# Attention on one core: VectorE's order by hand, P.V in three blocks of six key tiles, maxima moved by F32R matmuls

## The chip, the cores and the metric

The kernel runs on one core of a Trainium2 chip (8 cores, one used here). The metric is the device time of one execution in microseconds (us), as the median of repeated runs; lower is better. The engines of a core are TensorE (PE in the profile, its weight loads apart as PEld), VectorE (DVE), ScalarE (ACT), GpSimd (POOL) and SyncE (SP, which only issues transfers here). Each has its own queue and runs it in order; they meet at semaphores.

## The reference, cut to what matters

The whole computation is a two-layer backbone on 2048 latent and 256 context tokens: an RWKV-7 layer, then a latent-attention layer. The change touches the softmax attention of the second layer alone, 16 heads, 2048 queries against 2304 keys:

```python
def attend(q, k, v):        # q: 2048 x 16 x 96, k: 2304 x 16 x 96, v: 2304 x 16 x 64
    s = jnp.einsum('bqhd,bkhd->bhqk', q, k, preferred_element_type=jnp.float32) * (1.0 / math.sqrt(QK_NOPE + QK_ROPE))
    p = jax.nn.softmax(s, axis=-1).astype(v.dtype)
    return jnp.einsum('bhqk,bkhd->bqhd', p, v, preferred_element_type=jnp.float32).astype(q.dtype)
...
d_x = (o * jax.nn.silu(g_x)) @ w_out
```

Everything is float32. The kernel keeps that precision by splitting operands into a high and a low F32R part (F32R is a float32 format that TensorE takes in one pass) and adding products.

## The kernel before

`attention` works on 32 **groups**: 8 pairs of heads (`p`) times 4 blocks of 512 queries (`g`). The list `work` holds them in order. In a group a loop runs over 18 key tiles of 128 keys (`kt`). For each key tile `scores` (L1699) issues five pairs of matmuls into `ps_s` (two buffers), one matmul of a pair for each head, and ScalarE takes the exponential into a tile `pt` (L1708; nine buffers). Called **S** below.

The maxima that softmax subtracts are found one group ahead. `prepass` (L1668) is a generator that `next(bg, None)` advances: each of its 18 **units** (called **U**) multiplies queries by 512 keys into two `ps_p` tiles, one for each head (three buffers of `ps_p` in all), and VectorE reduces each to a maximum (L1684, L1686). After the 18 units VectorE reduces to `zm` (L1688), eight small float32 matmuls turn those columns into rows (L1694, called **M**), and ScalarE and then VectorE copy one row each into `qr2` (L1697). The last of the five score matmul pairs of the next group reads `qr2`, which is how the maximum is subtracted.

P.V is `av(st, n)` (L1724): the next `n` key tiles of the group, two float32 matmuls each, accumulated in the one buffer of `ps_o`. The group's calls are five tiles at `kt` 6, five at `kt` 11, six after the loop, and the last two in `finish_group` (L1790), which runs inside the next group at `kt` 1.

The row sums of the exponentials are added up elementwise by two engines in `accumulate` (L1711): VectorE adds key tiles 1, 3, 7, 11 and 15 into `acc1` (four instructions), GpSimd the other thirteen into `acc0` (twelve), and then GpSimd adds `acc1` to `acc0` (L1832). `finish_group` calls `av`, `scaled` (multiplies P.V by the gate, L1733) and `sums` (L1735): two matmuls with ones sum `acc0` over the keys, ScalarE copies the result (L1742), VectorE takes the reciprocal in four pieces of 128 columns (L1745) and multiplies (L1747), and SP sends the result off.

What sets the order: `manual_schedule(engines={PE})` keeps TensorE's instructions in the order in which the code is written. VectorE, ScalarE, GpSimd and SP are ordered by the scheduler of the language at build time, by its own priorities. [...] A buffer that is still being read holds up the instruction that wants to write it: a unit needs two of the three `ps_p` buffers, and those come free by VectorE's reductions.

## Time and profile before

| | us |
|---|---|
| median of 3 runs | 5520.99 (5520.9 to 5532.2) |
| profiled execution | 5527.81 |
| its span, first to last instruction | 5526.0 |
| one steady group of attention, from its first S to the next group's | 52.84 |
| last group, from its first S to its sums | 46.05 |

| engine over the span | busy us | share |
|---|---|---|
| PE | 4724.3 | 85% |
| DVE | 3784.7 | 68% |
| POOL | 2752.4 | 50% |
| ACT | 2186.3 | 40% |

Attention lies between about 3620 and 5325 us of the span; what lies ahead of it (RWKV, projections) and behind it (the output product and the final norm) is not touched. The busy shares are means over all stages. What an edit in attention is worth has to be read from a group: it repeats 32 times with nearly the same timing, so one of them, from 4525.33 to 4578.17, is read closely. In the timeline a row gives the start, the time until the last instruction of the row ended, and how many instructions it merges; since matmuls overlap, the distance of two starts is what a step costs.

### The profile page before, as it was taken

What the parts mean: (1) busy time and instruction counts of PE and PEld (TensorE: products, weight loads), DVE (VectorE), ACT (ScalarE), POOL (GpSimd) and SP (SyncE); (2) the same over time, 40 slices, a digit from 0 to 9 for tenths busy, and PEclk for the clock granted to TensorE, in tenths of its full rate; (3) what the DMA queues carried; (4) which work ended last, traced back from release to release, by engine and by line L of the source; (5) the groups of instructions that cost most, each with busy time, mean ns of one, the idle gap of its engine ahead of it and who ended that gap; (6) DMA issues with size and microseconds to landing.
All of it is one profiled execution on the core that took longest, in us unless ns stands there. A gap on an engine that the chain in (4) does not pass through costs nothing.

```text
span 5526.0 us, 123424 instructions
## 1 busy us (share of the span) xinstructions
PE 4724.3 (85%) x50559; PEld 3434.1 (62%) x50559; DVE 3784.7 (68%) x6213; ACT 2186.3 (40%) x3862; POOL 2752.4 (50%) x2473
## 2 busy tenths in 40 slices
PE   6778787887878887677789998699999999999999
PEld 4655555555767776466667876555555555555567
DVE  5989897875888888786565443266666666666644
ACT  4444444443544444333333343233333333333332
POOL 2575656463544444343254452255656655656551
PEclk8889898887989999788889999889999999999999
DMA  7655555556776666868788767621111111011023
GB/s 220 188 168 171 162 165 172 165 169 188 212 214 175 186 178 168 243 196 235 229 247 256 246 163 237 235 76 54 30 50 58 28 51 57 23 58 32 25 91 104
DMA packets 1006881, 818.59 MB, mean 148 GB/s; under 512 B 280885, under 2 KB 876420, under 8 KB 994794
## 3 DMA queue, kind: packets, MB, share of 16 engines
q1 hardware_dynamic: 872046, 734.48, 44.5%
q10 hardware_dynamic: 134188, 75.95, 5.0%
q8 instruction: 397, 6.50, 0.5%
q14 instruction: 170, 1.39, 0.1%
q0 software_dynamic: 80, 0.26, 0.0%
HBM read 551.84 MB, written 258.66 MB: 147 GB/s over the span
## 4 chain that ended last, share of the span: by engine, by line
PE 31%; DVE 9%; DMA 3%; ACT 2%; issue 2%; POOL 2%; SPq 1%; ACTq 0%; DVEq 0%; POOLq 0%
PE ps_o L1729 9%; PE ps_s L1706 7%; PE ps_p L1680 4%; DVE mx L1684 3%; DVE ri L1745 2%; DVE acc L1722 1%; PE ps_a L1387 1%; PE ps_a L1388 1%; PE ps_a L1389 1%; ACT pt L1708 1%; PE ps_o L1882 1%; PE ps_o L1884 1%; PE ps_o L1883 1%; DVE acc L1719 1%; PE ps_p L1694 1%
## 5 line engine op out<-in xcount | busy, mean ns | idle before, releaser
L1722 POOL TENSOR_TENSOR acc<-acc,pt 128x1024 f32<-128x1024 f32 x352 | 867.2, 2464 | 406.5 <-ACT pt L1708 386.5
L1684 DVE TENSOR_REDUCE mx<-ps_p 128x1 f32<-128x512 f32 x1024 | 661.5, 682 | 356.8 <-PE ps_p L1680 356.7
L1708 ACT ACTIVATE pt<-ps_s 128x1024 f32<-128x1024 f32 x576 | 591.0, 1026 | 779.8 <-PE ps_s L1706 737.6
L1706 PE MATMUL ps_s<-qr,a_kr 64*128 64x512 f32 (+1 forms) x2304 | 524.6, 393 | 5.8 <-ACT qr L1697 4.0
L1729 PE MATMUL ps_o<-pt,av 128*64 128x512 f32 x2304 | 523.3, 599 | 0.0
L1680 PE MATMUL ps_p<-knh,qnh 64*128 64x512 f32 (+1 forms) x1280 | 369.9, 404 | 99.3 <-DVE mx L1684 48.9
L500 PE MATMUL ps_r<-lh,whi 128*128 128x512 f32 (+1 forms) x960 | 386.4, 404 | 37.0 <-ACT lh L492 33.4
L418 POOL TENSOR_TENSOR wlo<-wraw,whi 128x1024 fp32r<-128x1024 f32 (+3 forms) x120 | 265.7, 2215 | 300.2 <-ACT whi L414 293.8
L501 PE MATMUL ps_r<-ll,whi 128*128 128x512 f32 (+1 forms) x960 | 382.7, 400 | 15.4 <-DVE ll L493 11.9
L502 PE MATMUL ps_r<-lh,wlo 128*128 128x512 f32 (+1 forms) x960 | 379.6, 397 | 12.9 <-POOL wlo L418 7.1
L696 POOL TENSOR_TENSOR f_wlo<-f_wraw,f_whi 128x384 fp32r<-128x384 f32 x118 | 158.8, 1347 | 384.4 <-ACT f_whi L694 320.0
L1729 PEld LDWEIGHTS ps_o<-pt,av 128*64 128x64 f32 x2304 | 154.3, 137 | 296.3 <-issue 292.2
L1680 PE MATMUL ps_p<-a_kr,qr 64*128 64x512 f32 (+1 forms) x1280 | 329.5, 391 | 1.5 <-DMA qr<-qr 1.5
L1706 PEld LDWEIGHTS ps_s<-qr,a_kr 64*128 64x128 f32 (+1 forms) x2304 | 289.9, 185 | 64.3 <-DVE qr L1697 15.2
L1680 PEld LDWEIGHTS ps_p<-knh,qnh 64*128 64x128 f32 x1280 | 184.3, 189 | 196.8 <-DVE mx L1684 132.2
L480 DVE SCALAR_TENSOR_TENSOR lerp<-xx,cols,hb 128x512 f32<-128x512 f32 (+1 forms) x240 | 239.3, 1022 | 88.2 <-POOL ll L493 67.9
L1706 PE MATMUL ps_s<-qnh,knl 64*128 64x512 f32 x1152 | 283.0, 417 | 4.3 <-ACT pt L1708 4.2
L1150 PE MATMUL ps_s<-svu,big 128*64 128x64 f32 x4544 | 236.7, 247 | 52.0 <-DVE svu L1138 30.3
L1706 PE MATMUL ps_s<-qnh,knh 64*128 64x512 f32 x1152 | 267.5, 389 | 0.0
L1706 PE MATMUL ps_s<-qnl,knh 64*128 64x512 f32 x1152 | 267.4, 389 | 0.0
L1097 DVE TENSOR_TENSOR big<-ps_aa,amask 64x256 f32<-64x256 f32 x576 | 243.2, 422 | 29.7 <-PE ps_aa L1092 16.3
L1110 ACT COPY big<-ps_aa 64x256 f32<-64x256 f32 x576 | 211.0, 366 | 132.2 <-PE ps_aa L1106 126.2
(342 smaller groups left out, 12550.1 us busy)
## 6 DMA issues: line engine op xcount, KB each, us to landing
f_w<-wod SPq DMA_DIRECT2D x72, 1024.0 KB
wraw<-rwkv_w_in SPq DMA_DIRECT2D x120, 512.0 KB
kbt<-KB SPq DMA_DIRECT2D x72, 512.0 KB
big<-AR SPq DMA_DIRECT2D x144, 256.0 KB
AR<-ar SPq DMA_DIRECT2D x64, 512.0 KB
KB<-kb SPq DMA_DIRECT2D x64, 512.0 KB
f_wraw<-rwkv_w_in SPq DMA_DIRECT2D x64, 512.0 KB
f_wraw<-mla_w_in SPq DMA_DIRECT2D x54, 512.0 KB
```

What stands on the lines that cost most here:

```text
L418: eng.tensor_tensor(lo[:, k0:k1, :], raw[:, k0:k1, :], hi[:, k0:k1, :].bitcast(F32), ALU.subtract)
L480: nc.vector.scalar_tensor_tensor(L[:, :W], xx[:, k, :W], col["mu"][:, j * 8 + k:j * 8 + k + 1], hb[:, k, 1:W + 1], ALU.mult, ALU.add)
L500: nc.tensor.matmul(ps, hi[:, k, :], lh[k][:, :W], start=k == 0, stop=False)
L501: nc.tensor.matmul(ps, hi[:, k, :], ll[k][:, :W], start=False, stop=False)
L502: nc.tensor.matmul(ps, lo[:, k, :], lh[k][:, :W], start=False, stop=k == KT - 1)
L1097: nc.vector.tensor_tensor(B[r, 2 * p0 + e::4, 0, ck], ps[e][o], amask[o, d:d + 1, :].to_broadcast([64, 4, 64]), ALU.mult)
L1680: nc.tensor.matmul(ps[h2][:, o * kw:(o + 1) * kw], x[r, t * P:(t + 1) * P], y[r, k0:k0 + kw], start=st, stop=not st)
L1684: nc.vector.tensor_reduce(mx[:, h2, t, n % 4:n % 4 + 1], ps[h2], mybir.AxisListType.X, ALU.max)
L1706: nc.tensor.matmul(ps[:, h2, :], x[r, ks], y[r, :], start=i == 0, stop=i == 4)
L1708: nc.scalar.activation(pt, ps, AF.Exp, scale=SCALE)
L1722: eng.tensor_tensor(a, a, pt, ALU.add)
L1729: nc.tensor.matmul(st["po"][hs, :], st["v"][:, kt, hs], pt[:, h2, :], start=kt == 0, stop=kt == NK - 1)
```

## The change

- VectorE joins TensorE in `manual_schedule`: its instructions now keep the order of the code.
- P.V comes in three blocks of six key tiles: at `kt` 7, at `kt` 13 and, for the last six, at `kt` 1 of the next group. Behind each block one more unit of the prepass is issued, so that its 18 units end at `kt` 14 and M comes at `kt` 16 of the same group.
- `sums` of the group before moves from `kt` 1 to `kt` 7, just ahead of the block there. ScalarE's copy goes; VectorE takes one reciprocal of 512 columns straight from PSUM.
- VectorE adds only key tiles 10, 11 and 12 (two instructions), at `kt` 13 in front of the block there. GpSimd adds the other fifteen (fourteen instructions) and then `acc1`. `acc1` has one buffer in place of two.
- M: `zm` becomes a tile of 4 x 128 columns, zero but for two columns of each 128 (two such tiles, cleared once by GpSimd), and four F32R matmuls with an F32R identity (`a_idr`) replace the eight float32 ones.

```diff
@@ -1639,10 +1639,16 @@
             qp = es2.enter_context(tc.tile_pool(name="at_q", bufs=2))
             tp = es2.enter_context(tc.tile_pool(name="at_t", bufs=2))
             pp = es2.enter_context(tc.tile_pool(name="at_ps", bufs=1, space=PSUM))
-            es2.enter_context(tc.manual_schedule(engines={mybir.EngineType.PE}))
+            es2.enter_context(tc.manual_schedule(engines={mybir.EngineType.PE, mybir.EngineType.DVE}))
             wl = cp.tile([P, KT - WC, 2, D], F32R, name="a_wl")
             ones = rp.tile([P, 64], F32, name="a_ones")
             nc.vector.memset(ones, 1.0)
+            idr = rp.tile([P, P], F32R, name="a_idr")
+            nc.vector.tensor_copy(idr, self.ident)
+            zms = [rp.tile([P, 4, P], F32R, name=f"zm{i}") for i in range(2)]
+            for z in zms:
+                nc.gpsimd.memset(z.bitcast(F32), 0.0)
+            zms = itertools.cycle(zms)
             kr1 = rp.tile([P, T], F32R, name="a_kr1")
             kr2 = rp.tile([P, T], F32R, name="a_kr2")
 
@@ -1667,7 +1673,7 @@
 
             def prepass(q, k):
                 qnh, _, qr1, qr2 = q
-                z = tp.tile([P, 8], F32, name="zm")
+                z = next(zms)
                 mx = tp.tile([P, 2, 4, 5], F32, name="mx")
                 units = [[(t, j * 512, 512)] for t in range(4) for j in range(4)]
                 units += [[(t, 2048, 256), (t + 1, 2048, 256)] for t in (0, 2)]
@@ -1685,13 +1691,11 @@
                         else:
                             nc.vector.tensor_reduce(mx[:, h2, t:t + 2, 4], ps[h2].rearrange("p (t k) -> p t k", t=2), mybir.AxisListType.X, ALU.max)
                     yield
-                nc.vector.tensor_reduce(z, mx.rearrange("p h t j -> p (h t) j"), mybir.AxisListType.X, ALU.max, negate=True)
+                nc.vector.tensor_reduce(z[:, :, 32::64].rearrange("p t h -> p h t"), mx, mybir.AxisListType.X, ALU.max, negate=True)
                 yield
                 pz = pp.tile([P, 512], F32, name="ps_p", bufs=3)
                 for t in range(4):
-                    for h2 in range(2):
-                        o = 32 + 64 * h2
-                        nc.tensor.matmul(pz[o:o + 1, t * P:(t + 1) * P], z[:, 4 * h2 + t:4 * h2 + t + 1], self.ident, start=True, stop=True)
+                    nc.tensor.matmul(pz[:, t * P:(t + 1) * P], z[:, t, :], idr, start=True, stop=True)
                 for h2 in range(2):
                     o = 32 + 64 * h2
                     (nc.vector.tensor_copy if h2 else nc.scalar.copy)(qr2[o:o + 1, :], pz[o:o + 1, :])
@@ -1708,18 +1712,16 @@
                 nc.scalar.activation(pt, ps, AF.Exp, scale=SCALE)
                 return pt
 
-            def accumulate(st, kt, pt):
-                if kt < 2:
-                    st["first"].append(pt)
-                    return
-                j = 1 if kt % 4 == 3 else 0
-                eng = nc.vector if j else nc.gpsimd
-                if j not in st["acc"]:
-                    a = st["acc"][j] = tp.tile([P, 2, QG], F32, name=f"acc{j}")
-                    eng.tensor_tensor(a, st["first"][j], pt, ALU.add)
-                else:
-                    a = st["acc"][j]
-                    eng.tensor_tensor(a, a, pt, ALU.add)
+            def add(st, eng, j, *pts):
+                for pt in pts:
+                    a = st["acc"].get(j)
+                    if a is None:
+                        a = st["acc"][j] = tp.tile([P, 2, QG], F32, name=f"acc{j}", bufs=2 - j)
+                        st["first"][j] = pt
+                    elif j in st["first"]:
+                        eng.tensor_tensor(a, st["first"].pop(j), pt, ALU.add)
+                    else:
+                        eng.tensor_tensor(a, a, pt, ALU.add)
 
             def av(st, n):
                 for _ in range(n):
@@ -1739,10 +1741,7 @@
                 for h2 in range(2):
                     nc.tensor.matmul(psm[h2 * 64:(h2 + 1) * 64, :], ones, a[:, h2, :], start=True, stop=True)
                 ri = tp.tile([P, QG], F32, name="ri", bufs=1)
-                nc.scalar.copy(ri, psm)
-                for i in range(4):
-                    c = slice(i * P, (i + 1) * P)
-                    nc.vector.reciprocal(ri[:, c], ri[:, c])
+                nc.vector.reciprocal(ri, psm)
                 ot = st["ot"]
                 nc.vector.tensor_tensor(ot, ot, ri, ALU.mult)
                 (nc.sync if (p, g) != (NP - 1, NG - 1) else nc.gpsimd).dma_start(self.oT[p, :, g * QG:(g + 1) * QG], ot)
...
 
-            def finish_group(st):
-                av(st, len(st["pend"]))
-                scaled(st)
-                sums(st)
-
             for i, (p, g) in enumerate(work):
                 q, k, v = nq, kv, kv[2]
                 gt = tp.tile([P, QG], F32, name="gt")
                 nc.sync.dma_start(gt, self.mG[p, :, g * QG:(g + 1) * QG])
-                st = {"pg": (p, g), "v": v, "gt": gt, "pend": [], "first": [], "acc": {}}
+                st = {"pg": (p, g), "v": v, "gt": gt, "pend": [], "first": {}, "acc": {}}
                 bg = iter(())
                 if i + 1 < len(work):
                     if g + 1 == NG:
@@ -1806,11 +1800,14 @@
                 for kt in range(NK):
                     pt = scores(kt, q, k)
                     st["pend"].append((kt, pt))
-                    accumulate(st, kt, pt)
+                    if kt not in (10, 11, 12):
+                        add(st, nc.gpsimd, 0, pt)
                     next(bg, None)
                     if kt == 1:
                         if prev:
-                            finish_group(prev)
+                            av(prev, 6)
+                            scaled(prev)
+                            next(bg, None)
                         if i + 2 < len(work):
                             fq = load_q(*work[i + 2])
                     if kt == 2 and g == 0:
@@ -1824,17 +1821,23 @@
                             wg = wout_split(range(WC))
                     if kt >= 3:
                         next(wg, None)
-                    if kt == 6:
+                    if kt == 7:
+                        if prev:
+                            sums(prev)
                         st["po"] = pp.tile([P, QG], F32, name="ps_o")
-                        av(st, 5)
-                    if kt == 11:
-                        av(st, 5)
+                        av(st, 6)
+                        next(bg, None)
+                    if kt == 13:
+                        add(st, nc.vector, 1, *(x[1] for x in st["pend"] if x[0] in (10, 11, 12)))
+                        av(st, 6)
+                        next(bg, None)
                 nc.gpsimd.tensor_tensor(st["acc"][0], st["acc"][0], st["acc"][1], ALU.add)
-                av(st, 6)
                 for _ in bg:
                     pass
                 prev = st
-            finish_group(prev)
+            av(prev, 6)
+            scaled(prev)
+            sums(prev)
             for _ in wg:
                 pass
             es2.close()
```

VectorE in the middle of attention, before: one group in the order in which it runs. `mx` is the prepass's maxima, `acc` the sums of exponentials, `ri` the reciprocal, `ot` the group's output.

```order
L1688 TENSOR_REDUCE zm<-mx 128x8
L1697 CAST qr_44048<-ps_p 1x512
L1684 TENSOR_REDUCE mx<-ps_p 128x1 x4
L1733 TENSOR_TENSOR ot<-ps_o,gt 128x512
L1745 RECIPROCAL ri<-ri 128x128 x4
L1684 TENSOR_REDUCE mx<-ps_p 128x1
L1747 TENSOR_TENSOR ot<-ot,ri 128x512
L1684 TENSOR_REDUCE mx<-ps_p 128x1 x2
L1719 TENSOR_TENSOR acc_45056<-pt 128x1024
L1684 TENSOR_REDUCE mx<-ps_p 128x1 x8
L1722 TENSOR_TENSOR acc_45056<-acc_45056,pt 128x1024
```

The same engine and place in the changed kernel:

```order
L1694 TENSOR_REDUCE zm_43773<-mx 128x2x4
L1701 CAST qr_44528<-ps_p 1x512
L1690 TENSOR_REDUCE mx<-ps_p 128x1 x4
L1735 TENSOR_TENSOR ot<-ps_o,gt 128x512
L1690 TENSOR_REDUCE mx<-ps_p 128x1 x14
L1744 RECIPROCAL ri<-ps_p 128x512
L1746 TENSOR_TENSOR ot<-ot,ri 128x512
L1690 TENSOR_REDUCE mx<-ps_p 128x1 x14
L1722 TENSOR_TENSOR acc_45765<-pt 128x1024
L1724 TENSOR_TENSOR acc_45765<-acc_45765,pt 128x1024
L1692 TENSOR_REDUCE mx<-ps_p 128x2 x4
```

The reciprocal moved from behind 4 reductions of a group to behind 18, and the adds, once spread among the reductions, now stand together behind the 32nd.

TensorE around the sums (`a_ones`), before. `ps_p<-knh,qnh` and the row behind it are one unit, the five `ps_s` rows one S.

```order
L1680 MATMUL ps_p<-knh,qnh 128x512 x2
L1680 MATMUL ps_p<-a_kr_43770,qr_47899 128x512 x2
L1729 MATMUL ps_o<-pt,av 64x512 x4
L1740 MATMUL ps_p<-acc_47919,a_ones 64x512 x2
L1706 MATMUL ps_s<-qnh,knl 128x512 x2
L1706 MATMUL ps_s<-qnl,knh 128x512 x2
L1706 MATMUL ps_s<-qr_47419,a_kr_43770 128x512 x2
L1706 MATMUL ps_s<-qnh,knh 128x512 x2
L1706 MATMUL ps_s<-qr_47420,a_kr_43771 128x512 x2
L1680 MATMUL ps_p<-knh,qnh 128x512 x2
```

TensorE around the sums in the changed kernel:

```order
L1686 MATMUL ps_p<-knh,qnh 128x512 x2
L1686 MATMUL ps_p<-a_kr_43776,qr_47830 128x512 x2
L1742 MATMUL ps_p<-acc_47774,a_ones 64x512 x2
L1731 MATMUL ps_o<-pt,av 64x512 x12
L1686 MATMUL ps_p<-knh,qnh 128x512 x2
L1686 MATMUL ps_p<-a_kr_43776,qr_47830 128x512 x2
L1710 MATMUL ps_s<-qnh,knl 128x512 x2
```

Behind the sums there now stands a block of twelve P.V matmuls, where an S and a unit stood.

TensorE around M in the changed kernel (before, M stood between the last P.V block of a group and the next group's first S):

```order
L1710 MATMUL ps_s<-qr_46418,a_kr_43777 128x512 x2
L1698 MATMUL ps_p<-a_idr,zm_43772 128x128 x4
L1710 MATMUL ps_s<-qnh,knl 128x512 x2
L1710 MATMUL ps_s<-qnl,knh 128x512 x2
L1710 MATMUL ps_s<-qr_46417,a_kr_43776 128x512 x2
L1710 MATMUL ps_s<-qnh,knh 128x512 x2
L1710 MATMUL ps_s<-qr_46418,a_kr_43777 128x512 x2
L1710 MATMUL ps_s<-qnh,knl 128x512 x2
```

M now has the whole last S of its group (`qr_46418`) between itself and the next group's first S.

## Rows read from the trace of the kernel before

**Rows 1.** The page: busy time, share and instructions of each engine.
```profile
PE 4724.3 (85%) x50559; PEld 3434.1 (62%) x50559; DVE 3784.7 (68%) x6213; ACT 2186.3 (40%) x3862; POOL 2752.4 (50%) x2473
```
**Rows 2.** All instructions of M: ns min/median/max, first and last start.
```profile
L1694 PE MATMUL ps_p<-ident,zm x512: 270/272/417, 3621.5 to 5270.0; 128*1 128x128 f32 x171
```
**Rows 3.** Two stretches: us, busy PE, PEld, DVE, ACT, POOL, clock, DMA, GB/s.
```profile
4525.33:4578.17 52.84, 50.80 (x355) 30.74 (x353) 34.94 (x48) 19.63 (x20) 31.78 (x14) 1.00 0.11 28
5270.17:5316.22 46.05, 42.52 (x267) 21.75 (x265) 15.62 (x12) 19.63 (x20) 34.92 (x14) 1.00 0.02 7
```
**Rows 4.** TensorE's timeline through the steady group: start, us, instructions, idle before.
```profile
4525.33 0.51 PE L1706 MATMUL ps_s<-qnh,knl 64*128 64x512 f32 x2
...
4529.32 1.94 PE L1729 MATMUL ps_o<-pt,av 128*64 128x512 f32 x8
...
4532.05 0.49 PE L1706 MATMUL ps_s<-qnh,knl 64*128 64x512 f32 x2
...
4536.77 0.49 PE L1680 MATMUL ps_p<-knh,qnh 64*128 64x512 f32 x1 [1.47 <-DVE mx L1684]
...
4543.40 4.51 PE L1729 MATMUL ps_o<-pt,av 128*64 128x512 f32 x20
4547.85 0.49 PE L1706 MATMUL ps_s<-qnh,knl 64*128 64x512 f32 x2
...
4556.86 4.51 PE L1729 MATMUL ps_o<-pt,av 128*64 128x512 f32 x20
4561.31 0.49 PE L1706 MATMUL ps_s<-qnh,knl 64*128 64x512 f32 x2
...
4563.03 0.39 PE L1706 MATMUL ps_s<-qnh,knl 64*128 64x512 f32 x2
...
4564.64 0.39 PE L1706 MATMUL ps_s<-qnh,knl 64*128 64x512 f32 x2
...
4571.90 5.37 PE L1729 MATMUL ps_o<-pt,av 128*64 128x512 f32 x24
4577.20 1.04 PE L1694 MATMUL ps_p<-ident,zm 128*1 128x128 f32 x16
4578.17 0.50 PE L1706 MATMUL ps_s<-qnh,knl 64*128 64x512 f32 x2
```
**Rows 5.** The chain of waits through the same group: start, us, what.
```profile
4525.44 0.59 ACT qr L1697
...
4526.06 0.71 DVE qr L1697
...
4532.16 0.60 ACT ri L1742
...
4532.78 3.39 DVE ri L1745 x4
```
**Rows 6.** VectorE's timeline, the same group.
```profile
4550.43 1.23 DVE L1722 TENSOR_TENSOR acc<-acc,pt 128x1024 f32<-128x1024 f32 x1
...
4557.62 2.92 DVE L1722 TENSOR_TENSOR acc<-acc,pt 128x1024 f32<-128x1024 f32 x1 [0.18 <-ACT pt L1708]
...
4564.84 1.29 DVE L1684 TENSOR_REDUCE mx<-ps_p 128x1 f32<-128x512 f32 x2 [0.32 <-PE ps_p L1680]
```
**Rows 7.** GpSimd's timeline, the same group.
```profile
4552.14 7.32 POOL L1722 TENSOR_TENSOR acc<-acc,pt 128x1024 f32<-128x1024 f32 x3 [4.95 <-ACT pt L1708]
```
**Rows 8.** All instructions on `acc`: ns min/median/max, first and last start.
```profile
L1722 POOL TENSOR_TENSOR acc<-acc,pt x352: 2347/2382/3256, 3641.2 to 5311.4; 128x1024 f32<-128x1024 f32 x176
...
L1722 DVE TENSOR_TENSOR acc<-acc,pt x96: 1224/1244/2975, 3653.4 to 5304.4; 128x1024 f32<-128x1024 f32 x96
```
**Rows 9.** All instructions on `ot`, the multiplication by the reciprocal.
```profile
L1747 DVE TENSOR_TENSOR ot<-ot,ri x32: 691/884/1348, 3692.4 to 5322.1; 128x512 f32<-128x512 f32 x32
```
**Rows 10.** Groups by form, VectorE: a reciprocal of 512 columns elsewhere in the kernel.
```profile
L1359 DVE RECIPROCAL mt<-mt 128x512 f32<-128x512 f32 x8 | 26.8, 3352 | 2.5 <-ACT mt L1358 2.5
```
**Rows 11.** TensorE's timeline at the end of attention: the last group's sums.
```profile
5316.22 1.83 PE L1740 MATMUL ps_p<-acc,a_ones 128*64 128x512 f32 x4 [3.37 <-POOL acc L1832]
```

## The prediction

> **What bounds the kernel now.** The page gives TensorE 85% of the span, VectorE 68%, GpSimd 50%, ScalarE 40% [rows 1]: TensorE leads, but a mean over stages prices nothing. So the next view is the instructions of M, one block of 16 in each of 32 groups: from the first start, 3621.5, to the last, 5270.0, lie 31 groups, 53.2 us each in the mean [rows 2]. The reader is to see that attention repeats, so that a saving counts 31 times. Third, the stretches: a steady group takes 52.84 us, with TensorE busy 50.80, VectorE 34.94, GpSimd 31.78, ScalarE 19.63, the granted clock at 1.00 (2.4 GHz) [rows 3]. Busy 50.80 looks like no room. The timeline shows that it is not so, because waiting matmuls are drawn long.
>
> I take the pace of undisturbed work from that timeline and lay it against the group. One S with its unit U takes 4564.64 - 4563.03 = **1.61**. A P.V block of five tiles takes 4547.85 - 4543.40 = 4.45, one of six 4577.20 - 4571.90 = **5.30**. M takes 4578.17 - 4577.20 = 0.97 [rows 4]. Between the blocks lie these stretches:
>
> - 4525.33 to 4529.32, two S+U: 3.99 for 3.22 of work, 0.77 lost.
> - 4532.05 to 4543.40, five S+U: 11.35 for 8.05, **3.30** lost.
> - 4547.85 to 4556.86, five: 9.01 for 8.05, 0.96 lost.
> - 4561.31 to 4571.90, six: 10.59 for 9.66, 0.93 lost.
>
> Together 5.96 us of 52.84 are not work. The chain of waits and the VectorE timeline name them. The 3.30: behind the sums ScalarE copies for 0.60 and VectorE takes four reciprocals for 3.39 [rows 5]; a unit's maxima stand behind them in VectorE's queue, so its `ps_p` buffers stay taken and TensorE waits for `mx` at 4536.77 [rows 4]; an add to `acc` follows. The 0.96 and 0.93: one VectorE add of about 1.23 in the middle of a stretch [rows 6]; VectorE needs 1.29 of every 1.61 for two reductions, so a delay is worked off slowly. The 0.77: the first S of a group waits for the two copies of the maxima, 0.59 on ScalarE and then 0.71 on VectorE [rows 5]. So the bound is TensorE's work plus holes made by VectorE's order; VectorE's 34.94 in total would fit.
>
> **The change part by part.**
>
> *The sums at `kt` 7 ahead of a block.* In VectorE's queue: two reductions of the unit before (done about 1.5 us after that unit ends, by the 0.32 of idle and 1.29 of [rows 6]), the reciprocal of 512 columns, 3.35 by the row of such an instruction [rows 10], and the multiplication, 0.69 to 1.35 [rows 9]. They end 5.5 to 6.2 after the unit. TensorE has in the same time the sums (0.96, from 4577.20 back: the two-tile block and the sums fill 4529.32 to 4532.05, and two tiles are 1.77) and the block (5.30): 6.26. The next unit's first result comes 0.5 later. So the reciprocal hides behind P.V, which asks nothing of VectorE. That the source is PSUM and not SBUF no row shows; 3.35 is the value taken, and up to 4.3 would still fit. Without the cover it would cost the 3.3 of today. ScalarE's copy of 0.60 goes from the path. Gain: **3.30**.
>
> *The three adds of VectorE in front of the block at `kt` 13.* Two instructions of 1.24 alone, up to 2.98 beside GpSimd [rows 8]: with the reductions ahead of them 1.5 + 2.5 = 4.0 to 7.5 after the unit, against 5.30 of block plus 0.5 of unit. GpSimd has one add, of tile 13, ready there, so one is held and one runs alone: 1.5 + 2.9 + 1.24 = 5.6. Hidden. The spread adds are gone: gain **0.96 + 0.93**.
>
> What the trace shows of a held add is the 2.92 us at 4557.62, while GpSimd's run of three adds lasts until 4559.46; from there it needs 1.08, and alone it takes 1.23 [rows 6, 7]. The Trainium skill, page "SBUF — State Buffer", section "Who interferes with whom", says that a VectorE instruction with two SBUF inputs contends with a GpSimd instruction that reads SBUF, the loser waiting for the whole instruction. The trace agrees; the rule speaks against this change, which fills GpSimd's queue, and what it would make of the time is the first rival.
>
> *M at `kt` 16.* 18 calls in the loop and three behind the blocks make 21; the 18 units end at `kt` 14, `zm` follows at 15, M at 16. Between M and the next group's first S lies the last S of the group. The two copies, 0.59 and 0.71 in a row, have that S (a unit is two of the seven matmul pairs in the 1.61, 0.46; an S is the other 1.15) and four fifths of the next to hide in. Gain: **0.77**. M itself: 16 passes at 0.97 today are 0.06 each. Four F32R matmuls could be four such passes, 0.24; a stationary operand of 128 columns in place of one could cost more, and I let it go to today's 0.97, or to nothing below. I take 0.5, halfway, as no row has this shape: gain **0.47**.
>
> *Blocks of six.* The work is the same 18 tiles. The first S behind a block today takes 4563.03 - 4561.31 = 1.72, that is 0.11 more than the pace [rows 4]; there are four such places in either kernel, so 0.44 of the 5.96 stays. Entering a block may cost as much: I leave 0.2.
>
> *GpSimd.* 15 instructions in place of 13, 2.38 each [rows 8]: 35.7 in a group of about 47, or 76%. Its last one must end before the sums at `kt` 7. Laid out by hand: the adds of tiles 14 to 17 and the final one start when tile 14's exponential is done, some 3 us before the group ends (three S, M), and take 11.9, so they end about 9 us into the next group; the sums stand at 18.7 (eight S+U are 12.9, the block 5.3, one unit 0.5). Ten us to spare. The same lag decides on the nine `pt` buffers: a tile's buffer is wanted nine tiles on, and GpSimd is at most six behind.
>
> *What remains.* VectorE's multiplication by the reciprocal has two SBUF inputs and now meets a GpSimd that rarely rests; held for up to one add, 2.4, it would end 0.9 to 1.0 late, of which a third is absorbed. I leave 0.35 a group.
>
> New group: 52.84 - 5.96 = 46.88, plus 0.44, minus 0.47, plus 0.2 and 0.35: **47.4**. Saving 5.44.
>
> *The ends.* 29 of the 31 groups are steady: 29 x 5.44 = 158. Two groups are longer (31 x 53.2 - 31 x 52.84 is about 11 together), by the weight splits on ScalarE and GpSimd that fall there; I leave those 11 untouched. The later of the two saves as the rest, 5.4; the first has no group before it, so no reciprocal, and I give it 2. The last group has no units and is bound by GpSimd: its sums waited 3.37 for the final add [rows 11], 46.05 after its first S [rows 3]. Now tile 14 comes behind fifteen S, three blocks and the sums, at about 36, and five instructions of 2.38 follow it, with about 1.2 of holds by VectorE: 49, 3 later than 46.05. Without ScalarE's copy 0.6 comes back: minus 2.4.
>
> Sum: 158 + 5.4 + 2 - 2.4 = **163**. On the profiled execution, 5527.8, that is 5365. That execution lies 6.8 above the median of the runs, 5521.0, of which nothing shows the place; against the median it is **5358**.
>
> **The rivals.**
>
> *VectorE is held by GpSimd (slower than the forecast, still faster than before).* Place: the two adds at `kt` 13 and the multiplication behind the reciprocal. If each waits for a whole GpSimd add of 2.38, the adds end 1.5 + 2 x 3.62 = 8.7 after the unit against 6.0 wanted, 2.7 late, and the multiplication 1.0 late. About 0.6 of it is absorbed, so 3.1 a group in place of the 0.35: saving 2.7, in all some 80, 5441. Halfway, with one add held, 5400. For it: the 2.92, and GpSimd's 76%. Against: GpSimd has only tile 13 to add there. The rule of the Trainium skill named above, taken in full, is this rival.
>
> *GpSimd becomes the bound (slower than before).* Place: the sums' matmuls at `kt` 7, in front of all that TensorE has behind them. 15 instructions must fit in a group. At 47.4 us that decides from 3.16 us an instruction, and the kernel gets slower than before from 52.84 / 15 = 3.52. At 3.6 a group takes 54.0, 1.2 more, 36 in all: 5557. For it: single adds took up to 3.256 [rows 8]. Against: the median is 2.382, and only three VectorE instructions a group can hold GpSimd.
>
> *The cover shifts the holes but does not close them (no change).* VectorE by hand is fixed to one order; if the reductions of the seven units between two blocks came late each time, 7 x 1.29 = 9.0 in 10.1 of TensorE's work, the stretches would keep some 5 us of waits. Against: four S+U in a row run at 1.61 with VectorE idle 0.32 before each pair [rows 6].
>
> **How the numbers follow.** The forecast, 5335 to 5385 with 5358 most likely: 0.68. The first rival, 5385 to 5445: 0.20. GpSimd as the bound and slower: 0.04. No change: 0.03. Better than 5335 (M for nothing, no hold at all: a group of 46.3, saving 6.5, 195 in all, 5326): 0.05. The range of 8 in 10 takes the forecast and the nearer half of the first rival, with a little below: 5332 to 5420. Faster by over 0.2%, about what a measurement of this kernel can tell from no change: 0.68 + 0.20 + 0.05 = 0.93; same 0.03; slower 0.04.
>
> **What would show it.** In the changed kernel's profile: steady groups of 47 to 48; TensorE's idle time for `mx` gone; the reciprocal one instruction of about 3.35, ended before the block at `kt` 7 does; VectorE's adds at 1.24 to 3; M at 0.2 to 1.0 with no wait for `qr` behind it; GpSimd near 36 to 38 a group and TensorE not waiting for `acc` except at the very end. Wrong would make it: a reciprocal from PSUM beyond 4.3, waits of S for ScalarE where no units stand between (`kt` 15 to 17), or `pt` buffers that come free late.

## The result and the profile after

The changed kernel takes **5362.2 us** (5361.6 to 5367.7, 4 runs) against 5520.9 (5517.4 to 5532.2, 4 runs): a ratio of 0.9711, 95% interval 0.9695 to 0.9728, 159 us faster. The forecast was 5358 in 5332 to 5420. Its profiled execution took 5361.6, with a span of 5359.8.

The page's engine line, which answers to [rows 1]:

```profile
PE 4623.4 (86%) x50175; PEld 3437.2 (64%) x50175; DVE 3726.7 (70%) x6054; ACT 2167.4 (40%) x3830; POOL 2885.2 (54%) x2539
```

Two stretches, the steady group from its first S to the next one's and the last group from its first S to its sums, as [rows 3]:

```profile
4473.97:4521.32 47.35, 47.35 (x342) 30.59 (x340) 33.05 (x44) 19.06 (x19) 36.03 (x16) 1.00 0.12 32
5100.30:5150.17 49.87, 45.36 (x283) 22.74 (x279) 11.54 (x7) 19.50 (x19) 46.28 (x19) 1.00 0.02 6
```

The steady group fell from 52.84 to 47.35; the forecast was 47.4. TensorE's timeline through it, as [rows 4]: M, the first pair of matmuls that reads the new maxima row, the next P.V block, the unit behind it, the sums with their block, the unit behind that, the third block and the last unit:

```profile
4472.13 0.66 PE L1698 MATMUL ps_p<-a_idr,zm 128*128 128x128 f32 x4
4474.89 0.44 PE L1710 MATMUL ps_s<-qr,a_kr 33*128 33x512 f32 x2
4477.37 5.37 PE L1731 MATMUL ps_o<-pt,av 128*64 128x512 f32 x24
4482.68 0.50 PE L1686 MATMUL ps_p<-knh,qnh 64*128 64x512 f32 x2
4493.05 1.08 PE L1742 MATMUL ps_p<-acc,a_ones 128*64 128x512 f32 x4
4499.21 0.50 PE L1686 MATMUL ps_p<-knh,qnh 64*128 64x512 f32 x2
4509.56 5.37 PE L1731 MATMUL ps_o<-pt,av 128*64 128x512 f32 x24
4514.86 0.39 PE L1686 MATMUL ps_p<-knh,qnh 64*128 64x256 f32 x2
```

From 4482.68 to 4493.05 lie one unit and six S+U: 10.37 us for 0.46 + 6 x 1.61 = 10.12 of work. From 4499.21 to 4509.56 lie the same: 10.35. The long stretch of [rows 4] that lost 3.30 has no successor; each stretch now loses 0.2 to 0.3. VectorE's timeline, as [rows 6], with its copy of the maxima row and then the second and third block:

```profile
4473.96 0.70 DVE L1701 CAST qr<-ps_p 1x512 fp32r<-1x512 f32 x1 [2.51 <-ACT qr L1701]
4493.12 1.29 DVE L1690 TENSOR_REDUCE mx<-ps_p 128x1 f32<-128x512 f32 x2 [0.32 <-PE ps_p L1686]
4494.33 3.35 DVE L1744 RECIPROCAL ri<-ps_p 128x512 f32<-128x512 f32 x1
4497.71 0.90 DVE L1746 TENSOR_TENSOR ot<-ot,ri 128x512 f32<-128x512 f32 x1
4499.98 1.29 DVE L1690 TENSOR_REDUCE mx<-ps_p 128x1 f32<-128x512 f32 x2 [1.36 <-PE ps_p L1686]
4510.86 3.01 DVE L1722 TENSOR_TENSOR acc<-pt 128x1024 f32<-128x1024 f32 x1
4513.98 1.23 DVE L1724 TENSOR_TENSOR acc<-acc,pt 128x1024 f32<-128x1024 f32 x1
4515.64 1.29 DVE L1692 TENSOR_REDUCE mx<-ps_p 128x2 f32<-128x512 f32 x2 [0.43 <-PE ps_p L1686]
```

and, of GpSimd's timeline, the final add of the group before:

```profile
4480.53 2.35 POOL L1834 TENSOR_TENSOR acc<-acc,acc 128x1024 f32<-128x1024 f32 x1
```

Reciprocal and multiplication end at 4498.61, ahead of the block (4499.21), and VectorE then waits 1.36 for TensorE. Of the two adds one is held to 3.01 and one runs alone; behind them VectorE still waits 0.43. The copy of the maxima row ends at 4474.66, and the matmuls that read it start at 4474.89, in step with the pairs ahead of them. Around the blocks VectorE idles only for TensorE, and TensorE never waits for VectorE.

### The profile page after: what moved, and what is told of

It reads as the page before. It is cut to its first block, busy times and chain, and to the rows that moved or that the text cites. A ratio compares the mean times of both kernels' runs of the same rounds, so it can differ in the third digit from the quotient of the medians.

```text
span 5359.8 us, 122473 instructions
## 1 busy us (share of the span) xinstructions
PE 4623.4 (86%) x50175; PEld 3437.2 (64%) x50175; DVE 3726.7 (70%) x6054; ACT 2167.4 (40%) x3830; POOL 2885.2 (54%) x2539
## 5 line engine op out<-in xcount | busy, mean ns | idle before, releaser
L1724 POOL TENSOR_TENSOR acc<-acc,pt 128x1024 f32<-128x1024 f32 x416 | 1003.1, 2411 | 356.3 <-ACT pt L1712 333.6
L1710 PE MATMUL ps_s<-qr,a_kr 64*128 64x512 f32 (+1 forms) x2304 | 474.2, 392 | 0.3 <-DVE qr L1701 0.2
L1686 PE MATMUL ps_p<-knh,qnh 64*128 64x512 f32 (+1 forms) x1280 | 274.7, 399 | 37.4 <-DMA qnl<-qn 33.3
L1686 PE MATMUL ps_p<-a_kr,qr 64*128 64x512 f32 (+1 forms) x1280 | 260.4, 379 | 1.7 <-DMA qr<-qr 1.7
L1710 PEld LDWEIGHTS ps_s<-qr,a_kr 64*128 64x128 f32 (+1 forms) x2304 | 235.2, 185 | 38.4 <-DVE qr L1701 0.5
L500 PEld LDWEIGHTS ps_r<-lh,whi 128*128 128x128 f32 x960 | 197.7, 206 | 92.3 <-ACT lh L492 39.4
L1710 PE MATMUL ps_s<-qnh,knl 64*128 64x512 f32 x1152 | 241.0, 402 | 12.2 <-ACT pt L1712 12.0
L1150 PEld LDWEIGHTS ps_s<-svu,big 128*64 128x64 f32 x4544 | 193.9, 156 | 86.0 <-DVE svu L1138 40.9
L501 PEld LDWEIGHTS ps_r<-ll,whi 128*128 128x128 f32 x960 | 198.0, 206 | 59.6 <-DVE ll L493 19.7
```

Of the source, the lines that this page charges most:

```text
L500: nc.tensor.matmul(ps, hi[:, k, :], lh[k][:, :W], start=k == 0, stop=False)
L501: nc.tensor.matmul(ps, hi[:, k, :], ll[k][:, :W], start=False, stop=False)
L1150: nc.tensor.matmul(ps[e * 64:(e + 1) * 64, h // 2, :], B[:, h, 1, k:k + 64], S[:, e, h // 2, :], start=True, stop=True)
L1686: nc.tensor.matmul(ps[h2][:, o * kw:(o + 1) * kw], x[r, t * P:(t + 1) * P], y[r, k0:k0 + kw], start=st, stop=not st)
L1710: nc.tensor.matmul(ps[:, h2, :], x[r, ks], y[r, :], start=i == 0, stop=i == 4)
L1724: eng.tensor_tensor(a, a, pt, ALU.add)
```

## The experiments

The start of attention differs from run to run (the first M at 3615.3 in the changed kernel's trace, 3607.8 to 3626.1 in the eleven kernels below), and that comes from the program ahead of it. So the kernels are laid beside each other by their groups too, each from its first M to the next group's first M, worked out from the starts of M in each trace. 29 of the 31 intervals are regular; the first interval and the one of the first group of the last head pair (the "long" one) are not. "Group" is the mean of the regular intervals, "31 groups" the sum of all, and "tail" runs from the last M to the last sums.

```
kernel                       median us  ratio to before (95%)    group   31 groups  tail
before                        5520.9    -                         52.77   1647.7     47.0
changed                       5362.2    0.9711 (0.9695-0.9728)    47.38   1483.1     51.7
sums at key tile 4            5483.0    0.9927 (0.9913-0.9942)    51.23   1601.8     52.1
before, sums at tile 6        5467.9    0.9903 (0.9888-0.9918)    51.04   1593.1     47.0
VectorE's adds spread         5434.6    0.9844 (0.9828-0.9861)    49.78   1555.0     51.7
VectorE by the scheduler      5380.5    0.9744 (0.9730-0.9759)    48.00   1502.4     51.7
M behind the last tile        5405.6    0.9786 (0.9772-0.9799)    48.70   1521.3     51.3
M in float32                  5380.9    0.9742 (0.9729-0.9756)    47.82   1494.7     52.1
M both ways as before         5402.1    0.9779 (0.9764-0.9793)    48.79   1521.6     51.3
GpSimd adds all               5358.9    0.9704 (0.9691-0.9717)    47.30   1475.9     52.1
seven more GpSimd adds        5640.2    1.0214 (1.0199-1.0230)    55.45   1731.8     80.6
two reciprocals               5403.4    0.9788 (0.9772-0.9805)    48.86   1526.9     51.8
the ends mended               5336.2    0.9663 (0.9649-0.9676)    47.32   1464.7     47.2
```

### The sums without a block behind them

```diff
+                    if kt == 4 and prev:
+                        sums(prev)
                     if kt == 7:
-                        if prev:
-                            sums(prev)
```

> The changed kernel with one edit: the row sums and the reciprocal of the group before stand behind the prepass unit of key tile 4, with no P.V block behind them, instead of ahead of the block of key tile 7. Theory (the block behind the reciprocal is what hides it): VectorE is held 3.35 + 0.69 = 4.04 us in the middle of a stretch of units, and the two PSUM buffers that TensorE can still fill buy it 0.7 to 1.9 us; a hole of 2.1 to 3.3 us in each of 31 groups, 5427 to 5464 us, likeliest 5449. Rival (VectorE has 30% of its time free, so the place doesn't matter and the gain came from the larger blocks and the adds): 5362 us, no hole.

5483.0, 121 more, and 3.85 us more a group: above the range. TensorE's timeline behind the reciprocal:

```profile
4560.49 0.50 PE L1686 MATMUL ps_p<-knh,qnh 64*128 64x512 f32 x1 [0.68 <-DVE ri L1744]
4561.95 0.78 PE L1686 MATMUL ps_p<-knh,qnh 64*128 64x512 f32 x1 [0.96 <-DVE mx L1690]
```

Stretches of this place (columns as in [rows 3]), and below them two whole groups, M to M:

```profile
4556.80:4560.50 3.70, 3.02 (x27) 2.18 (x25) 3.67 (x3) 1.61 (x2) 3.62 (x2) 1.00 0.01 2
4562.50:4565.80 3.30, 3.30 (x19) 2.34 (x15) 1.41 (x3) 0.42 (x1) 3.22 (x2) 0.56 0.11 41
4386.47:4436.65 50.18, 48.55 (x343) 30.94 (x341) 32.86 (x43) 19.04 (x20) 35.97 (x16) 1.00 0.10 30
4539.75:4591.56 51.81, 50.17 (x343) 31.96 (x341) 32.88 (x43) 19.07 (x20) 35.94 (x16) 0.97 0.12 29
```

The wait named by the theory is there: first for the reciprocal's buffer, then for `mx`. In 8 of the 29 regular groups the clock stays at 1.00 and the group takes 50.0 to 50.3, 2.8 more than 47.38: inside the 2.1 to 3.3. In the other 21 the granted clock falls after TensorE has stood still twice for under 1 us, in the group shown to 0.56 over the next 3.3 us, nearly the lower of its two levels (1.2 GHz); such groups take 51.4 to 51.8. So the block hides the reciprocal, and without it the hole costs 2.8 us, and in most groups half as much again by the clock.

### The sums alone, in the kernel before

```diff
                         if prev:
-                            finish_group(prev)
+                            av(prev, len(prev["pend"]))
+                            scaled(prev)
...
                     if kt == 6:
+                        if prev:
+                            sums(prev)
```

> The kernel before with one edit: row sums and reciprocals moved from behind the block of key tile 1 to ahead of its block of key tile 6 (five tiles, about 4.4 us). Theory: the hole of 3.30 us goes, but the first VectorE add now stands alone between reductions and costs about 1.0 as its two fellows do; 2.3 x 31 = 71 us less, 5450 us (5419 if the add stays hidden). Rival (the sums' place brings nothing without the hand-made order): 5521 us.

5467.9 against 5522.5 in the same comparison: 55 less, 1.73 a group where 2.3 stood. The timelines of VectorE and, in the second row, of TensorE, with its one idle time in the stretch ahead of the sums:

```profile
4501.09 1.85 DVE L1719 TENSOR_TENSOR acc<-pt 128x1024 f32<-128x1024 f32 x1
4503.60 1.09 PE L1680 MATMUL ps_p<-knh,qnh 64*128 64x512 f32 x2 [0.45 <-DVE mx L1684]
4508.23 3.39 DVE L1745 RECIPROCAL ri<-ri 128x128 f32<-128x128 f32 x4 [0.58 <-ACT ri L1742]
4511.65 0.69 DVE L1747 TENSOR_TENSOR ot<-ot,ri 128x512 f32<-128x512 f32 x1
```

The reciprocals are covered even by the block of five, and the first add, which used to lie in their hole, now makes one of its own: the stretch from 4496.90 to 4506.49, five S+U or 8.05 us of work, still loses 1.54 where it lost 3.30. So the place of the sums is worth 1.7 us as long as the adds stand where they stood.

### VectorE's adds, spread or left to the scheduler

```diff
                     if kt not in (10, 11, 12):
                         add(st, nc.gpsimd, 0, pt)
+                    else:
+                        add(st, nc.vector, 1, pt)
...
                     if kt == 13:
-                        add(st, nc.vector, 1, *(x[1] for x in st["pend"] if x[0] in (10, 11, 12)))
```

> The changed kernel with one edit: VectorE's two adds stand behind key tiles 11 and 12, each ahead of the reductions of that tile's unit, instead of both ahead of the block of key tile 13. Theory: each costs the 0.9 to 1.0 us that such adds cost in the kernel before, 1.9 x 32 = 61 us, 5421 us; if GpSimd holds the first one for 2.9 us here too, 3.5 x 32 = 112, 5474. Rival (it is the smaller number of adds that pays, not their place): 5362 us.

5434.6: 72 more, 2.40 a group, 1.2 for each add in the mean, where 0.9 to 1.0 was expected. In the regular groups no add was held. VectorE's timeline shows a delay that the theory left out: ahead of the first add VectorE stands idle for an exponential, with the unit's reductions queued behind it:

```profile
4495.89 1.25 DVE L1722 TENSOR_TENSOR acc<-pt 128x1024 f32<-128x1024 f32 x1 [0.98 <-ACT pt L1712]
```

and the list of waits (total us, times, longest) the effect:

```profile
PE ps_p L1686 <- DVE mx L1690: 47.9, 58, 1.5
```

58 waits of TensorE are two in each of 29 groups. In the other kernel VectorE is taken out of the hand-made order:

```diff
-            es2.enter_context(tc.manual_schedule(engines={mybir.EngineType.PE, mybir.EngineType.DVE}))
+            es2.enter_context(tc.manual_schedule(engines={mybir.EngineType.PE}))
```

> The changed kernel with VectorE's order left to the scheduler again, all else as it is. In the order that the scheduler makes, only the two adds move: the first stands one unit, the second half a place earlier, ahead of the reductions of the units of key tiles 12 and 13. Theory: the first add makes a hole of 0.9 (alone) to 2.6 us (held by GpSimd), the second is still covered by the block that follows: 29 to 83 us more, 5391 to 5445 us, likeliest 5392. Rival (the hand-made order is only a matter of form): 5362 us.

5380.5: 18 more, 0.62 a group, below the range.

```profile
4464.29 1.21 DVE L1722 TENSOR_TENSOR acc<-pt 128x1024 f32<-128x1024 f32 x1
4465.43 1.28 DVE L1690 TENSOR_REDUCE mx<-ps_p 128x1 f32<-128x512 f32 x2
4466.62 1.21 DVE L1724 TENSOR_TENSOR acc<-acc,pt 128x1024 f32<-128x1024 f32 x1
```

Both adds run alone here, and the hole of the first is only 0.6, since its backlog is carried into the block a unit later. So the hand-made order is worth 19 of the 164.5 us that the 31 intervals gained; the changed code, left to the scheduler, gets the others.

### The maxima matmuls

```diff
                 nc.vector.tensor_reduce(z[:, :, 32::64]..., ALU.max, negate=True)
                 yield
+                yield
                 pz = ...
```

> The changed kernel with one edit: the maxima matmuls stand behind the last key tile of the group instead of one key tile earlier, so that the first scores of the next group follow them at once. Theory: these wait for the two copies of the maxima row, 0.77 us in each of 31 groups as in the kernel before: 24 us more, 5386 us. Rival (the wait is hidden by the four matmul pairs that come before the one that needs the row): 5362 us.

5405.6: 43 more; by the groups 38, 1.32 each instead of 0.77. The timelines of ScalarE (two rows), VectorE and TensorE behind M, which started at 4506.05:

```profile
4506.22 1.03 ACT L1713 ACTIVATE pt<-ps_s 128x1024 f32<-128x1024 f32 x1 [0.43 <-PE ps_s L1711]
4507.28 0.58 ACT L1702 CAST qr<-ps_p 1x512 fp32r<-1x512 f32 x1
4507.89 0.70 DVE L1702 CAST qr<-ps_p 1x512 fp32r<-1x512 f32 x1 [4.00 <-ACT qr L1702]
4508.64 0.50 PE L1711 MATMUL ps_s<-qr,a_kr 33*128 33x512 f32 x1 [0.23 <-DVE qr L1702]
```

The exponential of the group's last tile stands ahead of the copy in ScalarE's queue. In the kernel before, a block of six lay between that tile and M, and the exponential had long ended.

```diff
-                z = next(zms)
+                z = tp.tile([P, 8], F32, name="zm")
...
-                    nc.tensor.matmul(pz[:, t * P:(t + 1) * P], z[:, t, :], idr, start=True, stop=True)
+                    for h2 in range(2):
+                        o = 32 + 64 * h2
+                        nc.tensor.matmul(pz[o:o + 1, t * P:(t + 1) * P], z[:, 4 * h2 + t:4 * h2 + t + 1], self.ident, start=True, stop=True)
```

> The changed kernel with one edit: the maxima matmuls are the eight float32 ones of the kernel before again, at the new place. Theory: 0.97 us instead of 0.59 on TensorE, 0.38 x 31 = 12 us more, 5374 us. Rival (TensorE has slack at that place): 5362 us.

5380.9: the medians lie 19 apart, and the 31 intervals account for 11.6 of it, as expected (12). Then both together:

> The changed kernel with both edits of the maxima matmuls undone: eight float32 matmuls, and behind the last key tile. What is left of the change is VectorE's part. Theory (the two parts add up): groups of 47.36 + 1.30 + 0.37 = 49.0 us, as far as the single edits measured; 31 x 1.67 = 52 us more, 5414 us. Rival (the two overlap, since the longer matmuls give the last exponential time to leave ScalarE ahead of the copy of the row): 48.6 us a group, 5401 us.

5402.1, 48.79 a group: the time is the rival's (5401), the group lies halfway between the two (49.0 and 48.6). The two edits cost 1.32 and 0.44 singly and 1.41 together, so they overlap by 0.35. All of the change but M thus brings 52.77 - 48.79 = 3.98 a group, and M's two parts up to 1.41, some 0.5 of which is a wait that the kernel before did not have. The cost of undoing one part is no share of the gain: the sums (2.8 at the full clock), the adds (2.40) and M (1.41) make 6.6, and the whole change brought 5.39. Blocks of six in place of five were not tried by themselves.

### Who holds whom: GpSimd

```diff
-                    if kt not in (10, 11, 12):
+                    if True:
                         add(st, nc.gpsimd, 0, pt)
...
-                nc.gpsimd.tensor_tensor(st["acc"][0], st["acc"][0], st["acc"][1], ALU.add)
```

> The changed kernel with one edit: GpSimd adds all 18 tiles of a group in 17 instructions, VectorE adds none and the final add of the two parts falls away. GpSimd then has 17 x 2.38 = 40.5 us of work in a group of 47.35. Theory (the held adds of VectorE are hidden and GpSimd is no bound): the 31 groups take what they take, the tail grows by two instructions, 4.8 us: 5367 us. Rival (VectorE held by GpSimd still costs something in each group): shorter groups; at 0.35 us each 5356 us. Rival (GpSimd is already the bound above 15 instructions): 31 x 2 x 2.38 more, 5510 us.

5358.9 (5352.4 to 5367.3): not to be told from the changed kernel. The regular groups take 47.30, 0.08 less; GpSimd is busy 40.8 of them:

```profile
4371.94:4419.22 47.28, 47.28 (x343) 30.48 (x341) 28.90 (x41) 19.08 (x20) 40.78 (x18) 1.00 0.34 106
```

TensorE waits for neither engine in the regular groups of this kernel, and VectorE without any add gains nothing, so its held adds cost nothing. The tail, for which 4.8 more were expected, grew by 0.4: in the changed kernel GpSimd has to wait out tiles 10 to 12 there, and starts the group with a final add that this kernel lacks. Now more work for GpSimd:

```diff
+                        if 2 <= kt < 9:
+                            nc.gpsimd.tensor_tensor(tp.tile([P, 2, QG], F32, name="dum", bufs=1), st["acc"][0], pt, ALU.add)
```

> The changed kernel with seven more adds a group on GpSimd (behind key tiles 2 to 8, into a tile that nobody reads): 22 instructions of 2.38 us, 52.4 us a group, against 47.36 that TensorE needs. Theory (GpSimd becomes the bound only above 47.36 us of work): groups of 52.4 us, 31 x 5.0 = 156 us more, 5518 us. Rival (the adds of GpSimd are off the path, and its queue is caught up somewhere): 5362 to 5380 us. The run of the kernel in which GpSimd had 40.8 us of work a group showed no loss.

5640.2, 278 more, 249 of it in the 31 intervals (groups of 55.45 in the mean) and 29 in the tail: GpSimd is the bound, and dearer than expected. One group, and two of GpSimd's adds in another:

```profile
4492.51:4550.72 58.21, 52.54 (x343) 32.90 (x341) 35.65 (x43) 20.01 (x20) 56.49 (x24) 0.88 0.27 86
4430.86 3.22 POOL L1724 TENSOR_TENSOR acc<-acc,pt 128x1024 f32<-128x1024 f32 x1
4434.16 3.24 POOL L1806 TENSOR_TENSOR dum<-acc,pt 128x1024 f32<-128x1024 f32 x1
```

and the list of waits:

```profile
ACT pt L1712 <- POOL dum L1806: 210.8, 65, 7.4
PE ps_s L1710 <- ACT pt L1712: 139.1, 64, 7.5
```

From one group's first add to the next one's (4408.40 to 4464.34), GpSimd does 22 adds in 55.94 without rest, 2.54 each: 2.44 from start to start where nothing holds it, and 3.2 to 3.3 for the two that meet VectorE's adds, shown above. TensorE waits for the exponential, which waits for a `pt` buffer that GpSimd has yet to read. The sums are not where it bites.

### How much the block hides

```diff
+                nc.vector.reciprocal(tp.tile([P, QG], F32, name="ri2", bufs=1), psm)
                 nc.vector.reciprocal(ri, psm)
```

> The changed kernel with a second reciprocal of the same row sums in front of the first, its result unused: 6.7 us of VectorE ahead of a block of 5.3. Theory (the block hides what fits under it, and VectorE had 1.36 us to spare in the trace of the changed kernel): a hole of 3.35 - 1.36 = 2.0 us in each of 31 groups, 62 us, 5424 us; where the hole is long enough for the granted clock to fall, as it did behind the reciprocal put at key tile 4, up to 1.65 more, 5475 us. Rival (the block hides nothing to spare): 3.35 x 31 = 104 us, 5466 us, at a full clock. Rival (any length is hidden): 5362 us.

5403.4: 41 more; 1.48 a group, with the granted clock at 1.00 in the regular groups. So 3.35 - 1.48 = 1.9 us were to spare, half a microsecond more than VectorE's idle time of 1.36 shows:

```profile
4413.63 3.35 DVE L1744 RECIPROCAL ri<-ps_p 128x512 f32<-128x512 f32 x1
4416.90 3.29 DVE L1745 RECIPROCAL ri<-ps_p 128x512 f32<-128x512 f32 x1
4420.84 2.57 DVE L1690 TENSOR_REDUCE mx<-ps_p 128x1 f32<-128x512 f32 x4
```

The four reductions in one row are the reason: TensorE had already filled the first unit's buffers, and part of the next one's, and VectorE works the backlog off without its pauses.

### A version that beats both: the ends

```diff
-                        raw = tp.tile([P, 512], F32, name="wraw")
+                        raw = tp.tile([P, 512], F32, name="wraw", bufs=4)
...
-                    if kt not in (10, 11, 12):
+                    if kt not in (10, 11, 12) and not (i + 1 == len(work) and kt > 9):
                         add(st, nc.gpsimd, 0, pt)
+                    elif i + 1 == len(work):
+                        add(st, nc.vector, 1, pt)
...
-                nc.gpsimd.tensor_tensor(st["acc"][0], ...
+                (nc.gpsimd if i + 1 < len(work) else nc.vector).tensor_tensor(st["acc"][0], ...
```

> The changed kernel with two edits off the regular groups: the buffer of the raw output weights has four instances instead of two, and in the last group, which has no prepass, VectorE adds key tiles 10 to 17 and the final sum, GpSimd tiles 0 to 9. Theory: the long group loses most of its 10.7 us excess, since ScalarE's exponentials no longer queue behind casts that wait for a transfer, which waits for a buffer that GpSimd's split frees (about 9 us), and the 4.4 us wait ahead of the last row sums goes: 5362 - 13 = 5349 us. Rival (the casts wait for the transfers themselves, and the tail waits for the last exponential): within 3 us of 5362.

**5336.2** (5332.9 to 5340.8), 0.9663 of the kernel before, 0.9649 to 0.9676, where the changed kernel has 0.9711, 0.9695 to 0.9728: 26 us less, where 13 were expected. The changed kernel's timelines of GpSimd, SyncE's queue and ScalarE in the long group, then a stretch of that group (columns as in [rows 3]), and in the last row TensorE's timeline at the end of attention (as [rows 11]):

```profile
4951.48 1.29 POOL L1290 TENSOR_TENSOR knl<-wraw,knh 128x512 fp32r<-128x512 f32 x1
4952.74 2.35 POOL L1724 TENSOR_TENSOR acc<-acc,pt 128x1024 f32<-128x1024 f32 x1
4952.80 11.05 SPq L1764 DMA_DIRECT2D wraw<-mla_w_out  x4
4955.39 0.62 ACT L1289 CAST knh<-wraw 128x512 fp32r<-128x512 f32 x1 [4.81 <-DMA wraw<-mla_w_out]
4966.44 0.62 ACT L1289 CAST av<-wraw 128x512 fp32r<-128x512 f32 x1 [3.26 <-DMA wraw<-mla_w_out]
4963.40:4973.60 10.20, 5.57 (x26) 4.44 (x28) 1.29 (x2) 3.48 (x4) 7.62 (x6) 0.50 0.17 51
5150.17 1.08 PE L1742 MATMUL ps_p<-acc,a_ones 128*64 128x512 f32 x4 [4.37 <-POOL acc L1834]
```

Four casts wait 13.1 us in all for transfers that wait for a buffer, which GpSimd's split frees from behind an add; the exponentials queue behind the casts, and TensorE's scores wait 7.7 for one of them, until 4968.03. From within that wait the granted clock is at 0.50 (1.2 GHz) until 4973.6, and the two S+U behind it take 5.90 in place of 3.22. The wait and the clock, 7.7 + 2.7, are nearly all of the 10.7 by which this group is longer than the others. With four buffers, three casts run in a row, and the clock stays at 1.00:

```profile
4935.10 1.65 ACT L1289 CAST knh<-wraw 128x512 fp32r<-128x512 f32 x3
```

and the last group, first S to sums, ends without that wait:

```profile
5076.35:5121.93 45.58, 45.45 (x284) 23.15 (x282) 18.20 (x12) 19.70 (x20) 31.50 (x13) 1.00 0.02 7
```

The long interval goes from 58.1 to 48.4, the first, which the theory had left out, from 51.0 to 44.0 (the same casts stand there), the tail from 51.7 to 47.2: 21 us of the 28.6 between the two spans (5359.8 and 5331.2). 5.2 of the rest lie ahead of the first M.

## Why the prediction held, step by step

*The bound: TensorE's work plus holes made by VectorE's order.* Right. The sum put a group at 47.4; it took 47.35 to 47.38. Every edit that gave VectorE work back between two units brought a hole (0.6 to 1.5 for an add, 2.8 for the reciprocal at the full clock), and taking all adds from VectorE brought nothing.

*The sums at `kt` 7, 3.30.* The mechanism was right. The reciprocal from PSUM took 3.35, the value taken. Laid out by hand its cover left about 1 us (4.3 would fit); 1.9 could be added. The step left out that TensorE also has a unit's buffers to fill before it stands still.

*The adds, 0.96 + 0.93, at 5.6 behind the unit.* Right: one held at 3.01, one alone at 1.23, hidden with 0.43 left.

*M, 0.77 + 0.47.* No wait for `qr` stands behind it. M takes 4472.72 - 4472.13 = 0.59, not 0.5: 0.38 gained instead of 0.47, and the single edit cost 0.44. Its place is worth 1.32 in the new layout, more than the 0.77 it replaced.

*Blocks and hold, 0.44 + 0.2 + 0.35.* What remains beside the work is 47.35 - (18 x 1.61 + 3 x 5.30 + 0.96 + 0.59) = 0.92, against 0.99 put in. But all of it is the way into and out of blocks and M; the 0.35 for a held multiplication wasn't needed, since it had 0.60 to spare ahead of the block's end. A low term for the blocks and a needless one for the hold made up for each other: that the group came out at 47.4 is luck by these 0.3 us.

*GpSimd, and its layout by hand.* Right: the final add ended at 4482.88, 8.9 us into the next group (about 9 was said) and the sums stand 19.1 in (18.7).

*The ends.* Here single terms failed and their sum did not:

```
                    predicted   measured
29 regular groups     158         156.3
first interval          2           7.6
later long interval     5.4         0.7
the end of attention   -2.4        -3.3
sum                   163         161.2
```

The first interval: the step forgot that four tiles of P.V, 3.5 us, and the S behind M, 1.15, pass out of it into the groups that follow. In the end the last group has them, and there TensorE waits 4.37 us for GpSimd anyway, so that the four tiles cost nothing. The long one: it was taken to save what the others save, but its time is set by the chain of casts, transfers and splits shown above and by the clock behind it, which the change doesn't touch; ahead of the splits GpSimd now has more adds. The four buffers, which break that chain, brought 9.7 there. The tail was bound by GpSimd as forecast: sums 49.87 after the first S, for 49. The -3.3 runs from the last M to the last multiplication (53.6 and 56.9 us); counted from the last group's first S, as the forecast did, it is the -2.4 that was said (52.65 and 55.08). That the four rows add up to within 2 us of the forecast is luck: the first interval saved 5.6 more than was said, the three other rows 7.3 less.

*The reference time.* Of the 6.8 us by which the profiled execution of before lay above the median nothing was known. Its attention began 6.2 later than the changed kernel's; starts spread over 18 us among all traces. Measured against the median the saving is 159, against the profiled execution 166, and attention itself gave 161.

*The rivals.* VectorE held by GpSimd: one add of two is held in each group, as far as the forecast went and no further, and without those adds the group is 0.08 shorter, so this rival gets nothing. Adds take 3.0 to 3.3 beside GpSimd's and 1.2 alone, and in the kernel with 22 adds GpSimd's own rise from 2.4 to 3.2. The Trainium skill, page "SBUF — State Buffer", section "Who interferes with whom", says that a VectorE instruction with two SBUF inputs contends with a GpSimd instruction that reads SBUF. The traces agree. GpSimd as the bound: 40.8 us of work a group cost nothing, and at 55.9 the groups took 55.5, as long as GpSimd, which fits a point of decision at the 47.4 of TensorE, though no run lies between; but the place was wrong, `pt` buffers and not the sums, as the last sentence of the prediction had among its doubts. Holes that only shift: none is there.

What stays open: why the granted clock fell in 21 of 29 groups of the kernel with early sums and not in the 8 others, whose rows around the stall look alike.

## What to carry to other kernels

Where two engines hand each other small buffers, give the long and non-urgent instructions of the slower one a place where the faster one does long work that needs nothing from it, and add up what fits there. Price a group that looks irregular by its own chain of waits before giving it the savings of the regular ones. An instruction that the new order makes wait (a copy behind an exponential, an exponential behind a cast) can cost more than the one it replaces.

## What the runs showed of the hardware

Two stalls of 0.68 and 0.96 us, with one matmul between them, were followed by a granted clock of 0.56 over 3.3 us in the group shown, one of the 21 of 29 in which it fell; a wait of 7.7 us was followed by 0.50, as the long group shows; the hole of 3.30 in the kernel before, with a wait of 1.47 [rows 4], left it at 1.00 [rows 3]. Four F32R matmuls with 128 stationary and 128 moving columns take 0.59, or 0.15 each, more than twice the 0.06 of a pass of the float32 ones of one column. A reciprocal of 512 columns costs 3.35 from PSUM as from SBUF [rows 10].
